# 42 gathered tokens on three partitions each in place of 32 on four, in a hybrid decoder step on one core

## The chip, the cores and the metric

The kernel runs on one core of a Trainium2 chip. The metric is device time in microseconds (us) of one execution. Besides TensorE (PE, with its weight loads as PEld), the core has VectorE (DVE), ScalarE (ACT), GpSimd (POOL) and SyncE (SP), whose queue issues most of the transfers.

## The reference, cut to what matters

264 tokens (256 of a prompt, 8 new ones) go through an input projection, attention and a recurrence, an output projection and a layer norm. That gives x1, 264 tokens by 2048. The change lies in the expert mixer behind it. Each token picks, for each of 8 heads, 16 of 16384 experts, so 128 experts with a weight each:

```
e = take(i1, si // 16) * 128 + take(i2, si % 16)        # 8 heads x 16 experts for a token
g = softmax(sv)
act = gelu(einsum('nd,nhkd->nhk', x, u_tab[e]))
out = einsum('nhk,nhkd->nd', g * act, v_tab[e])
y = layer_norm(alpha * x1 + out)
```

u_tab and v_tab are 16384 x 2048 in float32, 134 MB each.

## The kernel before, in words

The mixer treats the tokens in two ways. The first ND = 232 are dense: both tables are streamed through in 128 blocks of 128 experts, products are made for all experts, and a matrix of gates (zero nearly everywhere) picks the right ones. The last NG = 32 tokens are gathered: each token sits on REP = 4 partitions, and each of these partitions fetches 32 of its token's 128 experts, a half row of 1024 numbers at a time.

**Dense work.** A block is split into a high part `hi` (ACT rounds it, L97) and the rest `lo` (DVE subtracts, L100), in halves of 128x1024. A step s of the main loop does `up(s)` (16 pairs of matmuls: the high weights against x1's high and low parts, L1178, then the low weights against the high part, L1179), and `down(v)` with v = s - 34 (16 such pairs, L1229 and L1230, against the gated activations W). With ND = 232 a pair streams 464 and 232 columns. The high and low parts of x1 lie in `x1s`, 264 columns each, of which `up` reads the first 232 of either.

**Order of a step.** DVE's program order is: sum of the last `up` (`act_sum`, L1188), `lo` of the first half of `down`'s block, four additions into x1 (L1237), `lo` of the second half, gate product (L1205, L1210), `lo` of the first half of the next `up` block, low part of W (L1216), `lo` of its second half, then gathered work. ACT's order is alike; it rounds W behind the gate product (L1212) and the next `up` block behind that. Four pairs of buffers take `hi` and `lo`, six take what the transfers bring.

**Stages.** s = 0 to 5 multiply x1 in float32 without a split (L916), s = 4 to 20 also build the dense gates (L1127), s = 21 to 33 have `up` alone, steps v = 0 to 93 have `up` and `down`, and v = 94 to 127 (`last_step`) have `down` alone, since all 128 `up` blocks are done. The layer norm ends the kernel.

**Gathered work.** `gathered()` is a generator. After each step v, `credit` grows by GRATE, and each whole unit runs the generator to its next `yield`. The first three turns load the expert numbers `exf`, the gates `gat` and the tokens `xrep`, and compute row numbers `eix`. Then each turn issues one indirect transfer of a 128x1024 tile (POOL, L1363) and consumes the tile issued three turns before: for u a product with the token and a sum (`dot`, L1381), then for v a scaled addition (`acc`, L1395). When all is through, 16 matmuls with `selM` add up the partitions of each token (L1400).

Of the kernel before, what the change touches and what calls it, by code (L numbers as in the profile page):

```python
# [18 lines left out]
NC_ = 16  # L19
SEQ = 256  # L20
NB = 8
T = SEQ + NB
NPG = 8
NG = 32
ND = T - NG
REP = 128 // NG
RAWB = 6

SEQS = "qqqqqqqqkkkkkkkkvvvvrrrrrrrrvvvvrrrrrrrr"
# [16 lines left out]
TRATE = 4  # L46
LEAD = 4
GWAIT = 2
GRATE = 1.5
GDELAY = 3  # L50
EPS = 1e-5
LAM0 = 0.8 - 0.6 * math.exp(-0.0)
# [4 lines left out]
def _build(tc, I, O):  # L57
    nc = tc.nc
    ctx = ExitStack()
    PS = bass.MemoryType.PSUM  # L60
    with ctx:
# [50 lines left out]
        def pmisc(shape):  # L112
            return psum.tile(shape, F32, name="misc", bufs=3)
# [65 lines left out]
        iota = cload("iota", [128, 128])  # L179
# [509 lines left out]
        x1, wo = x0, {}  # L689
# [72 lines left out]
        for u in range(2 * NC_):  # L762
# [3 lines left out]
            if u % 2 == 0:  # L766
# [3 lines left out]
                hi, lo = wo.pop(u // 2)  # L770
# [138 lines left out]
        for c in range(NC_):  # L909
            ln.center(c)  # L910

        x1s = big.tile([128, NC_, 2, T], F32R, name="A")
        first = [(ups.pop(k), pmm()) for k in (-16, -15)]

        def native(p, w, c, n=T):
# [14 lines left out]
        Gd = [dram.tile([128, 128, n], F32, name=f"Gd{a}") for a, n in blocks]  # L930
        Ed = dram.tile([SEQ - ND, 128], F32, name="Ed")
        gd = dram.tile([SEQ - ND, 128], F32, name="gd")
        Es = dram.tile([2, 64, 16], F32, name="Es")
        xgd = dram.tile([NG, DM], F32, name="xgd")
        tctx = ExitStack()
        tp_ = pool_in(tctx, "topk", 2)
# [119 lines left out]
        for m in range(2, 16):  # L1056
            k = m - 16
            load_u(k + 2)
            w = ups.pop(k)
            p = pmm()  # L1060
            for i in range(NC_):
                native(p, w, i)
            if m % 2 == 0:
                scores(m // 2 - 1)
            queries(m, p)
            if m < 10:

                for c in range(2 * (m - 2), 2 * (m - 2) + 2):
                    nc.scalar.copy(x1s[:, c, 0], x1[:, c, :])
                    nc.vector.tensor_tensor(x1s[:, c, 1], x1[:, c, :], x1s[:, c, 0], op=OP.subtract)  # L1070
            elif m < 14:
                rows_out(m - 10)

# [9 lines left out]
        def tokens(tt):  # L1083

            i1, i2, g = [a.rearrange("p h k -> p (h k)") for a in (*tops[tt].r, tops[tt].g)]
            tr = []
            for k, a in enumerate((i1, i2, g)):
                p = pmisc([128, 128])
                nc.tensor.transpose(p, a, ident)
                b = tw[0].tile([128, 128], F32, name=f"tr{k}", bufs=1)  # L1090
                nc.scalar.copy(b, p)
                tr.append(b)
            b = tw[0].tile([128, 128], F32, name="tr3", bufs=1)
            nc.scalar.activation(b, tr[1], AF.Copy, scale=-1.0)
            tr.append(b)
            if tt == 1:
                r0 = ND - 128
                ef = tp_.tile([128, 128], F32, name="efp", bufs=1)
                nc.vector.scalar_tensor_tensor(ef, i1, 128.0, i2, op0=OP.mult, op1=OP.add)
                nc.gpsimd.dma_start(Ed, ef[r0:128])  # L1100
                nc.gpsimd.dma_start(gd, g[r0:128])
            yield
            for bk, (a0, n) in enumerate(blocks):
                if a0 // 128 != tt:
                    continue
                st = tw[0].tile([128, 128, n], F32, name="stage")
                for t4 in range(0, n, 4):
                    t0 = a0 % 128 + t4
                    b = tw[0].tile([128, 4, 128], F32, name="gb", bufs=4)
                    if t4 % 8 == 0:  # L1110
                        for q in range(4):
                            nc.scalar.activation(b[:, q, :], iota, AF.Abs, bias=tr[3][:, t0 + q:t0 + q + 1])
                        nc.scalar.activation(b, b, AF.Relu, scale=-1.0, bias=1.0)
                    else:
                        nc.vector.tensor_tensor(b, iota[:, None, :].to_broadcast([128, 4, 128]),
                                                tr[1][:, t0:t0 + 4, None].to_broadcast([128, 4, 128]), op=OP.is_equal)
                    a = tw[0].tile([128, 4, 128], F32, name="ga", bufs=4)
                    for q in range(4):
                        nc.vector.tensor_scalar(a[:, q, :], iota, tr[0][:, t0 + q:t0 + q + 1], tr[2][:, t0 + q:t0 + q + 1],
                                                op0=OP.is_equal, op1=OP.mult)  # L1120
                    if len(prev) == 3:
                        prev.pop(0)()

                    def product(a=a, b=b, st=st, t4=t4, n=n, bk=bk):
                        p = psum.tile([128, 4, 128], F32, name="acc2")
                        for q in range(4):
                            nc.tensor.matmul(p[:, q, :], b[:, q, :], a[:, q, :], start=True, stop=True)  # L1127
                        nc.scalar.copy(st[:, :, t4:t4 + 4], p.rearrange("p t i -> p i t"))
                        if t4 + 4 == n:
                            nc.sync.dma_start(Gd[bk], st)  # L1130

                    prev.append(product)
                    yield

        def gates():
            for tt in range(2):
                yield from tokens(tt)
            while prev:
                prev.pop(0)()
                yield  # L1140

            top = Top(64, 1, "s", ex)
            both([top], [SS], 0)
            yield
            top.less()
            yield
            top.pick(0, 1)
            yield
            top.gate()
            yield  # L1150
            ef = ex.tile([64, 16], F32, name="ef")
            nc.vector.scalar_tensor_tensor(ef, top.r[0][:, 0], 128.0, top.r[1][:, 0], op0=OP.mult, op1=OP.add)
            nc.gpsimd.dma_start(Es[0], ef)
            nc.gpsimd.dma_start(Es[1], top.g[:, 0])


        I["v2"] = I["v"].rearrange("e (a d) -> (e a) d", a=2)
# [9 lines left out]
        def up(k, a=0, b=NC_):  # L1167
            w = ups[k]
            if a == 0:
                pu[k] = pmm([128, 2, ND])  # L1170
            p = pu[k]
            if k < NAT:
                for c in range(a, b):
                    native(p[:, 0], w, c, ND)
                return
            for c in range(a, b):
                hi, lo = w[c // 8]
                nc.tensor.matmul(p, hi[:, c % 8, :], x1s[:, c, :, :ND], start=c == 0, stop=False)  # L1178
                nc.tensor.matmul(p[:, 0, :], lo[:, c % 8, :], x1s[:, c, 0, :ND], start=False, stop=c == NC_ - 1)  # L1179

        def act_sum(k):
            p = pu.pop(k)
# [153 lines left out]
        gp = pool_in(ctx, "gath", 1)  # L1336


        eix = gp.tile([128, 2, NG], I32, name="eix")
        gat = gp.tile([128, NG], F32, name="gat")  # L1340

        def gathered():
            exf = gp.tile([128, NG], F32, name="exf")
            selM = cload("selM", [128, NG], pool=gp)
            xrep = gp.tile([128, DM], F32, name="xrep")
            for r in range(REP):
                a, b, c = r * NG, r * NG + SEQ - ND, (r + 1) * NG
                for k, (d, o) in enumerate(((Ed, exf), (gd, gat))):
                    nc.sync.dma_start(o[a:b], d[:, a:c])
                    nc.sync.dma_start(o[b:c].rearrange("t (h k) -> t h k", k=16),  # L1350
                                      Es[k].rearrange("(h t) k -> t h k", h=8)[:, a // 16:c // 16])
                nc.sync.dma_start(xrep[a:c], xgd)
            for _ in range(GWAIT):
                yield

            nc.vector.tensor_scalar(eix[:, 0], exf, 2.0, None, op0=OP.mult)
            nc.vector.tensor_scalar(eix[:, 1], exf, 2.0, 1.0, op0=OP.mult, op1=OP.add)
            dots = gp.tile([128, 2, NG], F32, name="dots")
            yield

            def rows(tab, a, j):
# [2 lines left out]
                                             in_offset=bass.IndirectOffsetOnAxis(ap=eix[:, a, j:j + 1], axis=0))  # L1364
                return t

            todo = [(j, a) for j in range(NG) for a in range(2)]

            def ahead(tab, use):
                got = []  # L1370
# [11 lines left out]
                                               accum_out=dots[:, a, j:j + 1])  # L1382

            yield from ahead(I["u"], dot)
            wts = gp.tile([128, NG], F32, name="wts")
            nc.vector.tensor_tensor(wts, dots[:, 0], dots[:, 1], op=OP.add)
            nc.scalar.activation(wts, wts, AF.Gelu_apprx_tanh)
            nc.vector.tensor_tensor(wts, wts, gat, op=OP.mult)
# [6 lines left out]
                    nc.vector.scalar_tensor_tensor(accg[:, cols], t, wts[:, j:j + 1], accg[:, cols], op0=OP.mult, op1=OP.add)  # L1395

            yield from ahead(I["v2"], acc)
            pf = pmisc([128, NC_, NG])
            for c in range(NC_):
                nc.tensor.matmul(pf[:, c, :], accg[:, c * 128:(c + 1) * 128], selM, start=True, stop=True)  # L1400
            nc.vector.tensor_tensor(x1[:, :, ND:], x1[:, :, ND:], pf, op=OP.add)

        gg = gathered()
        credit = 0.0
# [51 lines left out]
def _arrays(inp):  # L1456
# [51 lines left out]
    a["cn"] = (to & (g % 2 == 1)[:, None]).astype(f)  # L1508
    a["own"] = (r[:, None] % 32 == np.arange(16)[None, :]).astype(f)
    r = np.arange(128)  # L1510
    a["selM"] = (r[:, None] % NG == np.arange(NG)[None, :]).astype(f)
    return a


# [28 lines left out]
```

## Time and profile before

| what | value |
|---|---|
| median of 3 runs (lowest, highest) | 2092.59 us (2090.44, 2094.37) |
| the profiled execution's own time | 2093.76 us |
| its span, first to last instruction | 2092.0 us |
| busy: PE, PEld, DVE, ACT, POOL | 97%, 88%, 76%, 46%, 11% of the span |
| mean granted TensorE clock | 0.982 of 2.4 GHz; 1.00 in every stretch from 600 to 2000 us |
| DMA | 522 MB, 250 GB/s over the span |

On PE, `down` of v = 0 starts at 918.68 us and that of v = 94 at about 1888 us; `down` ends near 2065 us, and the layer norm closes the kernel. A matmul's recorded duration is longer than its place in the stream, since matmuls overlap in the pipeline; what a matmul costs is read from one start to the next. The same holds for DVE: two operations in a row overlap by about 0.08 us.

### The profile page before, as it was taken

What the parts mean: (1) busy time and instruction counts of PE and PEld (TensorE: products, weight loads), DVE (VectorE), ACT (ScalarE), POOL (GpSimd) and SP (SyncE); (2) the same over time, 40 slices, a digit from 0 to 9 for tenths busy, and PEclk for the clock granted to TensorE, in tenths of its full rate; (3) what the DMA queues carried; (4) which work ended last, traced back from release to release, by engine and by line L of the source; (5) the groups of instructions that cost most, each with busy time, mean ns of one, the idle gap of its engine ahead of it and who ended that gap; (6) DMA issues with size and microseconds to landing.
All of it is one profiled execution on the core that took longest, in us unless ns stands there. A gap on an engine that the chain in (4) does not pass through costs nothing.

```text
span 2092.0 us, 37216 instructions
## 1 busy us (share of the span) xinstructions
PE 2022.8 (97%) x13890; PEld 1835.9 (88%) x13890; DVE 1589.3 (76%) x3245; ACT 969.1 (46%) x1600; POOL 239.6 (11%) x211
## 2 busy tenths in 40 slices
PE   7999899889899999999999999999999999999995
PEld 7888777679788999999999999999999999999995
DVE  5534555665599789667888888888888888878887
ACT  4223554534311599554444444444444444444444
POOL 0000000002400000000111111111222122200014
PEclk9999899989999999999999999999999999999998
DMA  8799488655344477778888888887888888876661
GB/s 282 273 372 319 153 283 305 206 200 180 113 141 142 145 243 242 260 230 321 279 298 302 279 299 293 285 292 251 299 301 280 303 288 289 298 226 222 225 204 62
DMA packets 183623, 522.08 MB, mean 250 GB/s; under 512 B 28858, under 2 KB 61650, under 8 KB 181394
## 3 DMA queue, kind: packets, MB, share of 16 engines
q1 hardware_dynamic: 160400, 451.34, 63.0%
q0 software_dynamic: 18688, 67.41, 9.7%
q8 instruction: 109, 1.79, 0.3%
q10 hardware_dynamic: 4354, 0.96, 0.2%
q14 instruction: 72, 0.59, 0.1%
HBM read 499.65 MB, written 19.97 MB: 248 GB/s over the span
## 4 chain that ended last, share of the span: by engine, by line
PE 79%; DVE 4%; ACT 3%; issue 1%; DMA 1%; POOL 0%; SPq 0%; ACTq 0%; POOLq 0%; DVEq 0%
PE mm L1178 19%; PE acc L1229 18%; PE mm L1179 9%; PE acc L1230 9%; PE mm L916 7%; PE mm L1229 3%; PE acc L1127 2%; PE mm L294 2%; PE acc L632 1%; PE mm L1230 1%; PE mm L295 1%; PE mm L296 1%; PE mm L777 1%; PE misc L373 1%; ACT hi L97 1%
## 5 line engine op out<-in xcount | busy, mean ns | idle before, releaser
L100 DVE TENSOR_TENSOR lo<-raw,hi 128x1024 fp32r<-128x1024 f32 x326 | 397.3, 1225 | 292.8 <-ACT hi L97 287.9
L1178 PE MATMUL mm<-A,hi 128*128 128x464 f32 x1728 | 568.3, 380 | 0.0
L1229 PE MATMUL acc<-w,xl 128*128 128x464 f32 x1640 | 532.7, 376 | 0.0
L1179 PE MATMUL mm<-A,lo 128*128 128x232 f32 x1728 | 465.8, 270 | 0.7 <-DVE lo L100 0.7
L1230 PE MATMUL acc<-w,xl 128*128 128x232 f32 x1640 | 443.0, 270 | 0.0
L97 ACT CAST hi<-raw 128x1024 fp32r<-128x1024 f32 x326 | 329.3, 1045 | 180.1 <-PE mm L295 95.9
L97 ACT CAST xl<-raw 128x1024 fp32r<-128x1024 f32 x260 | 269.1, 1045 | 221.4 <-issue 181.7
L1178 PEld LDWEIGHTS mm<-A,hi 128*128 128x128 f32 x1728 | 324.6, 188 | 42.0
L100 DVE TENSOR_TENSOR xl<-raw,xl 128x1024 fp32r<-128x1024 f32 x260 | 317.3, 1229 | 31.4 <-ACT xl L97 28.8
L1229 PEld LDWEIGHTS acc<-w,xl 128*128 128x128 f32 x1640 | 307.8, 188 | 35.9
L1179 PEld LDWEIGHTS mm<-A,lo 128*128 128x128 f32 x1728 | 330.7, 191 | 0.9 <-DVE lo L100 0.9
L1230 PEld LDWEIGHTS acc<-w,xl 128*128 128x128 f32 x1640 | 312.7, 191 | 0.0
L1212 ACT CAST w<-ac 128x232 fp32r<-128x232 f32 x128 | 49.5, 386 | 335.8 <-DVE ac L1210 335.8
L1237 DVE TENSOR_TENSOR M<-M,acc 128x232 f32<-128x232 f32 x444 | 166.4, 392 | 30.0 <-PE acc L1230 22.4
L916 PE MATMUL mm<-M,raw 128*128 128x264 f32 (+1 forms) x704 | 155.4, 381 | 7.2 <-ACT M L871 7.2
L916 PEld LDWEIGHTS mm<-M,raw 128*128 128x128 f32 x704 | 133.8, 192 | 25.4 <-ACT M L871 7.7
L294 PE MATMUL mm<-xh,hi 128*128 128x264 f32 x448 | 142.0, 317 | 12.4 <-ACT hi L97 6.6
L296 PE MATMUL mm<-xh,lo 128*128 128x264 f32 x448 | 131.5, 294 | 0.5 <-DVE lo L100 0.5
L295 PE MATMUL mm<-xl,hi 128*128 128x264 f32 x448 | 131.1, 293 | 0.2 <-DVE xl L173 0.2
L1363 POOL DMA_INDIRECT ug<-in_u,eix x64 | 79.3, 1239 | 441.3 <-DVE ug L1381 349.2
L1363 POOL DMA_INDIRECT ug<-in_v,eix x64 | 85.8, 1340 | 377.5 <-DVE xrep L1395 308.5
L294 PEld LDWEIGHTS mm<-xh,hi 128*128 128x128 f32 x448 | 88.3, 197 | 42.1 <-issue 28.2
(360 smaller groups left out, 3168.0 us busy)
## 6 DMA issues: line engine op xcount, KB each, us to landing
raw<-in_uT SPq DMA_DIRECT2D x256, 512.0 KB
raw<-in_vt SPq DMA_DIRECT2D x256, 512.0 KB
raw<-in_w_in SPq DMA_DIRECT2D x74, 512.0 KB
cv<-in_ck SPq DMA_DIRECT2D x64, 512.0 KB
cv<-in_cv SPq DMA_DIRECT2D x64, 512.0 KB
raw<-in_wq SPq DMA_DIRECT2D x32, 512.0 KB
Gd<-stage SPq DMA_DIRECT2D x14, 1024.0 KB
gt<-Gd SPq DMA_DIRECT2D x224, 64.0 KB
```

The lines of the kernel that those rows point to most:

```text
L97: nc.scalar.copy(hi, raw)
L100: (eng or nc.vector).tensor_tensor(lo, raw, hi, op=OP.subtract)
L294: nc.tensor.matmul(p, hi, xh[:, c], start=c == 0, stop=False)
L295: nc.tensor.matmul(p, hi, xl[:, c], start=False, stop=False)
L296: nc.tensor.matmul(p, lo, xh[:, c], start=False, stop=c == NC_ - 1)
L916: nc.tensor.matmul(p, w[c // 8][:, c % 8, :], x1[:, c, :n], start=c == 0, stop=c == NC_ - 1)
L1178: nc.tensor.matmul(p, hi[:, c % 8, :], x1s[:, c, :, :ND], start=c == 0, stop=False)
L1179: nc.tensor.matmul(p[:, 0, :], lo[:, c % 8, :], x1s[:, c, 0, :ND], start=False, stop=c == NC_ - 1)
L1229: nc.tensor.matmul(p[:, :, :ND], hi[:, b % 8, :], w, start=i == 0, stop=False)
L1230: nc.tensor.matmul(p[:, 0, :ND], lo[:, b % 8, :], w[:, 0], start=False, stop=i == 7)
L1237: nc.vector.tensor_tensor(a, a, p[:, b, :ND], op=OP.add)
L1363: nc.gpsimd.indirect_dma_start(out=t, out_offset=None, in_=tab, in_offset=bass.IndirectOffsetOnAxis(ap=eix[:, a, j:j + 1], axis=0))
```

## The change

NG becomes 42 and ND 222. Each gathered token sits on three partitions (REP = 128 // 42), which fetch 43, 43 and 42 of its 128 experts; partitions 126 and 127 hold zeros. So the generator has 86 tiles for each table in place of 64, and GRATE goes from 1.5 to 1.7. `x1s` keeps 222 columns only, so that the high and low parts lie side by side.

```
-NG = 32
+NG = 42
 ND = T - NG
 REP = 128 // NG
+NJ = -(-128 // REP)
...
-GRATE = 1.5
+GRATE = 1.7
...
-        x1s = big.tile([128, NC_, 2, T], F32R, name="A")
+        x1s = big.tile([128, NC_, 2, ND], F32R, name="A")
...
-                    t0 = a0 % 128 + t4
+                    t0, w = a0 % 128 + t4, min(4, n - t4)
...
-            nc.gpsimd.dma_start(Es[0], ef)
-            nc.gpsimd.dma_start(Es[1], top.g[:, 0])
+            for k, t in enumerate((ef, top.g[:, 0])):
+                for h in range(8):
+                    nc.gpsimd.dma_start(Es[k][:, h * 16:(h + 1) * 16], t[h * 8:(h + 1) * 8])
...
-                nc.tensor.matmul(p, hi[:, c % 8, :], x1s[:, c, :, :ND], start=c == 0, stop=False)
+                nc.tensor.matmul(p, hi[:, c % 8, :], x1s[:, c], start=c == 0, stop=False)
...
-        eix = gp.tile([128, 2, NG], I32, name="eix")
-        gat = gp.tile([128, NG], F32, name="gat")
+        eix = gp.tile([128, 2, NJ], I32, name="eix")
+        gat = gp.tile([128, NJ], F32, name="gat")
...
+            for t in (exf, gat, xrep):
+                nc.gpsimd.memset(t, 0.0)
...
-            todo = [(j, a) for j in range(NG) for a in range(2)]
+            todo = [(j, a) for j in range(NJ) for a in range(2)]
...
-            pf = pmisc([128, NC_, NG])
-            for c in range(NC_):
-                nc.tensor.matmul(pf[:, c, :], accg[:, c * 128:(c + 1) * 128], selM, start=True, stop=True)
-            nc.vector.tensor_tensor(x1[:, :, ND:], x1[:, :, ND:], pf, op=OP.add)
+            for h in (0, 8):
+                pf = pmisc([128, 8, NG])
+                for c in range(8):
+                    nc.tensor.matmul(pf[:, c, :], accg[:, (h + c) * 128:(h + c + 1) * 128], selM, start=True, stop=True)
+                nc.vector.tensor_tensor(x1[:, h:h + 8, ND:], x1[:, h:h + 8, ND:], pf, op=OP.add)
```

DVE's order at the border between the last step with `up` (v = 93) and the first two of `last_step`, before the change (`mm` and `acc` are PSUM tiles, `M` is x1, `ac` the activations, `gt` the gates, `xl`, `lo` and `hi` parts of weights):

```order
L1216 TENSOR_TENSOR w<-ac,w 128x232
L100 TENSOR_TENSOR lo<-raw,hi 128x1024
L1188 TENSOR_TENSOR ac<-ac,mm 128x232
L1205 TENSOR_TENSOR ac<-ac,gt 128x224
L1210 TENSOR_TENSOR ac<-ac,gt 128x8
L1237 TENSOR_TENSOR M<-M,acc_20614 128x232 x2
L1237 TENSOR_TENSOR M<-M,acc_20631 128x232 x2
L1216 TENSOR_TENSOR w<-ac,w 128x232
L100 TENSOR_TENSOR xl<-raw,xl 128x1024 x2
```

And the same place on DVE after the change (`xrep<-ug,wts,xrep` is the scaled addition of a gathered tile):

```order
L1218 TENSOR_TENSOR w<-ac,w 128x222
L101 TENSOR_TENSOR lo<-raw,hi 128x1024
L1400 SCALAR_TENSOR_TENSOR xrep<-ug,wts,xrep 128x1024
L1190 TENSOR_TENSOR ac<-ac,mm 128x222
L1207 TENSOR_TENSOR ac<-ac,gt 128x208
L1212 TENSOR_TENSOR ac<-ac,gt 128x14
L1239 TENSOR_TENSOR M<-M,acc_20626 128x222 x2
L1239 TENSOR_TENSOR M<-M,acc_20643 128x222 x2
L1218 TENSOR_TENSOR w<-ac,w 128x222
L101 TENSOR_TENSOR xl<-raw,xl 128x1024 x2
L1400 SCALAR_TENSOR_TENSOR xrep<-ug,wts,xrep 128x1024 x2
```

Before, the gathered additions are over by v = 91 and none stands behind it; now they go on into `last_step`: two, two and one by turns in v = 94 to 106, 22 in all.

PE's order at the end of the gathered work, before (the 16 matmuls with `selM` stand behind `down(91)`, and an `up` follows):

```order
L1229 MATMUL acc_20420<-w,xl 128x2x232
L1230 MATMUL acc_20420<-w,xl 128x232
L1400 MATMUL misc<-c_selM,xrep 128x32 x16
L1178 MATMUL mm<-A,hi 128x464
L1179 MATMUL mm<-A,lo 128x232
```

And PE after the change (behind `down(107)`, and `down(108)` follows):

```order
L1231 MATMUL acc_21478<-w,xl 128x2x222
L1232 MATMUL acc_21478<-w,xl 128x222
L1406 MATMUL misc<-c_selM,xrep 128x42 x16
L1231 MATMUL mm<-w,hi 128x2x222
L1232 MATMUL mm<-w,lo 128x222
```

The sums over partitions moved from a step with `up` into the stretch without, and every matmul of a pair lost 20 or 10 columns.

## Rows read from the trace of the kernel before

**Rows 1.** Busy time of the engines by stretch (from:to, length, engines, clock, DMA share, GB/s)

```profile
1000.00:1400.00 400.00, 400.00 (x2482) 371.31 (x2481) 340.14 (x580) 190.82 (x273) 72.43 (x58) 1.00 0.86 293
1430.00:1840.00 410.00, 410.00 (x2542) 380.45 (x2541) 350.49 (x537) 195.80 (x279) 79.92 (x60) 1.00 0.86 292
1886.00:2047.00 161.00, 161.00 (x1003) 149.98 (x1003) 137.09 (x264) 70.73 (x88) 8.60 (x7) 1.00 0.64 214
```

**Rows 2.** Timeline of PE (start us, duration, instruction): borders of up and down

```profile
1326.71 0.38 PE L1178 MATMUL mm<-A,hi 128*128 128x464 f32 x1
...
1843.24 0.38 PE L1178 MATMUL mm<-A,hi 128*128 128x464 f32 x1
...
1848.32 0.27 PE L1179 MATMUL mm<-A,lo 128*128 128x232 f32 x1
1848.43 0.38 PE L1229 MATMUL acc<-w,xl 128*128 128x464 f32 x1
...
1853.56 0.38 PE L1178 MATMUL mm<-A,hi 128*128 128x464 f32 x1
```

**Rows 3.** Who waited for whom, 1000 to 1700 us (total us, times, longest)

```profile
DVE lo L100 <- ACT hi L97: 95.4, 68, 1.5
```

**Rows 4.** Timeline of DVE over one step with two dots (idle before in brackets)

```profile
1320.05 0.38 DVE L1205 TENSOR_TENSOR ac<-ac,gt 128x224 f32<-128x224 f32 x1
...
1321.92 1.23 DVE L100 TENSOR_TENSOR lo<-raw,hi 128x1024 fp32r<-128x1024 f32 x1 [1.40 <-ACT hi L97]
...
1324.51 1.22 DVE L1381 SCALAR_TENSOR_TENSOR ug<-ug,xrep 128x1024 f32<-128x1024 f32 x1
...
1325.65 1.22 DVE L1381 SCALAR_TENSOR_TENSOR ug<-ug,xrep 128x1024 f32<-128x1024 f32 x1
...
1326.80 0.39 DVE L1188 TENSOR_TENSOR ac<-ac,mm 128x232 f32<-128x232 f32 x1
...
1330.85 0.38 DVE L1205 TENSOR_TENSOR ac<-ac,gt 128x224 f32<-128x224 f32 x1
```

**Rows 5.** Timeline of DVE over one step with two scaled additions

```profile
1464.78 0.38 DVE L1205 TENSOR_TENSOR ac<-ac,gt 128x224 f32<-128x224 f32 x1
...
1469.22 2.48 DVE L1395 SCALAR_TENSOR_TENSOR xrep<-ug,wts,xrep 128x1024 f32<-128x1024 f32 x2
1471.62 0.39 DVE L1188 TENSOR_TENSOR ac<-ac,mm 128x232 f32<-128x232 f32 x1
...
1475.67 0.38 DVE L1205 TENSOR_TENSOR ac<-ac,gt 128x224 f32<-128x224 f32 x1
```

**Rows 6.** Timeline of DVE over one step of down alone

```profile
1989.31 0.38 DVE L1205 TENSOR_TENSOR ac<-ac,gt 128x224 f32<-128x224 f32 x1
...
1991.12 0.82 DVE L1237 TENSOR_TENSOR M<-M,acc 128x232 f32<-128x232 f32 x2 [0.61 <-PE acc L1230]
...
1994.44 0.38 DVE L1205 TENSOR_TENSOR ac<-ac,gt 128x224 f32<-128x224 f32 x1
```

**Rows 7.** Groups of PE instructions, 600 to 850 us (busy us, mean ns)

```profile
L1127 PE MATMUL acc<-ga,gb 128*128 128x128 f32 x464 | 57.0, 276 | 1.0 <-ACT stage L1128 1.0
...
L916 PE MATMUL mm<-M,raw 128*128 128x232 f32 x192 | 38.4, 360 | 0.0
```

**Rows 8.** Timeline of PE: the matmuls with selM, and what follows

```profile
1863.87 3.66 PE L1400 MATMUL misc<-c_selM,xrep 128*128 128x32 f32 x32
1867.36 0.45 PE L1178 MATMUL mm<-A,hi 128*128 128x464 f32 x1
```

**Rows 9.** Timeline of DVE: the row numbers of the gathered experts

```profile
934.43 0.18 DVE L1356 TENSOR_SCALAR eix<-exf 128x32 int32<-128x32 f32 x1 [2.38 <-DMA gat<-Es]
```

**Rows 10.** Groups of POOL instructions (busy us, mean ns)

```profile
L715 POOL MEMSET M<- 128x2080 f32 x1 | 1.8, 1847 | 12.0 <-DVE xl L173 12.0
```

**Rows 11.** Busy time by stretch: the input projection's transfers

```profile
100.00:200.00 100.00, 100.00 (x1233) 85.14 (x1231) 41.77 (x89) 24.20 (x50) 0.00 (x0) 1.00 0.96 346
```

**Rows 12.** Transfers 1000 to 1700 us, median us from issue to landing

```profile
ug<-in_u,eix POOLq DMA_INDIRECT x54, 6.9
```

More of the change, by code (lines that the diff above doesn't have):

```diff
@@ L932, in _build @@
         gd = dram.tile([SEQ - ND, 128], F32, name="gd")
-        Es = dram.tile([2, 64, 16], F32, name="Es")
+        Es = dram.tile([2, NB, 128], F32, name="Es")
         xgd = dram.tile([NG, DM], F32, name="xgd")
@@ L1068, in _build @@
                 for c in range(2 * (m - 2), 2 * (m - 2) + 2):
-                    nc.scalar.copy(x1s[:, c, 0], x1[:, c, :])
-                    nc.vector.tensor_tensor(x1s[:, c, 1], x1[:, c, :], x1s[:, c, 0], op=OP.subtract)
+                    nc.scalar.copy(x1s[:, c, 0], x1[:, c, :ND])
+                    nc.vector.tensor_tensor(x1s[:, c, 1], x1[:, c, :ND], x1s[:, c, 0], op=OP.subtract)
             elif m < 14:
@@ L1107, in tokens @@
                 for t4 in range(0, n, 4):
-                    t0 = a0 % 128 + t4
+                    t0, w = a0 % 128 + t4, min(4, n - t4)
                     b = tw[0].tile([128, 4, 128], F32, name="gb", bufs=4)
                     if t4 % 8 == 0:
-                        for q in range(4):
+                        for q in range(w):
                             nc.scalar.activation(b[:, q, :], iota, AF.Abs, bias=tr[3][:, t0 + q:t0 + q + 1])
-                        nc.scalar.activation(b, b, AF.Relu, scale=-1.0, bias=1.0)
+                        nc.scalar.activation(b[:, :w], b[:, :w], AF.Relu, scale=-1.0, bias=1.0)
                     else:
-                        nc.vector.tensor_tensor(b, iota[:, None, :].to_broadcast([128, 4, 128]),
-                                                tr[1][:, t0:t0 + 4, None].to_broadcast([128, 4, 128]), op=OP.is_equal)
+                        nc.vector.tensor_tensor(b[:, :w], iota[:, None, :].to_broadcast([128, w, 128]),
+                                                tr[1][:, t0:t0 + w, None].to_broadcast([128, w, 128]), op=OP.is_equal)
                     a = tw[0].tile([128, 4, 128], F32, name="ga", bufs=4)
-                    for q in range(4):
+                    for q in range(w):
                         nc.vector.tensor_scalar(a[:, q, :], iota, tr[0][:, t0 + q:t0 + q + 1], tr[2][:, t0 + q:t0 + q + 1],
@@ L1122, in tokens, with product @@
                         prev.pop(0)()
-                    def product(a=a, b=b, st=st, t4=t4, n=n, bk=bk):
+                    def product(a=a, b=b, st=st, t4=t4, w=w, n=n, bk=bk):
                         p = psum.tile([128, 4, 128], F32, name="acc2")
-                        for q in range(4):
+                        for q in range(w):
                             nc.tensor.matmul(p[:, q, :], b[:, q, :], a[:, q, :], start=True, stop=True)
-                        nc.scalar.copy(st[:, :, t4:t4 + 4], p.rearrange("p t i -> p i t"))
-                        if t4 + 4 == n:
+                        nc.scalar.copy(st[:, :, t4:t4 + w], p[:, :w].rearrange("p t i -> p i t"))
+                        if t4 + w == n:
                             nc.sync.dma_start(Gd[bk], st)
@@ L1177, in up @@
                 hi, lo = w[c // 8]
-                nc.tensor.matmul(p, hi[:, c % 8, :], x1s[:, c, :, :ND], start=c == 0, stop=False)
-                nc.tensor.matmul(p[:, 0, :], lo[:, c % 8, :], x1s[:, c, 0, :ND], start=False, stop=c == NC_ - 1)
+                nc.tensor.matmul(p, hi[:, c % 8, :], x1s[:, c], start=c == 0, stop=False)
+                nc.tensor.matmul(p[:, 0, :], lo[:, c % 8, :], x1s[:, c, 0], start=False, stop=c == NC_ - 1)
         def act_sum(k):
@@ L1336, in _build @@
         gp = pool_in(ctx, "gath", 1)
-        eix = gp.tile([128, 2, NG], I32, name="eix")
-        gat = gp.tile([128, NG], F32, name="gat")
+        eix = gp.tile([128, 2, NJ], I32, name="eix")
+        gat = gp.tile([128, NJ], F32, name="gat")
         def gathered():
-            exf = gp.tile([128, NG], F32, name="exf")
+            exf = gp.tile([128, NJ], F32, name="exf")
             selM = cload("selM", [128, NG], pool=gp)
             xrep = gp.tile([128, DM], F32, name="xrep")
+            for t in (exf, gat, xrep):
+                nc.gpsimd.memset(t, 0.0)
             for r in range(REP):
[L1347 to L1352, printed above, removed]
+                a, b, e = r * NG, r * NG + SEQ - ND, (r + 1) * NG
+                c, d = r * NJ, min((r + 1) * NJ, 128)
+                for k, (i, o) in enumerate(((Ed, exf), (gd, gat))):
+                    nc.sync.dma_start(o[a:b, :d - c], i[:, c:d])
+                    nc.sync.dma_start(o[b:e, :d - c], Es[k][:, c:d])
+                nc.sync.dma_start(xrep[a:e], xgd)
             for _ in range(GWAIT):
@@ L1357, in gathered @@
             nc.vector.tensor_scalar(eix[:, 1], exf, 2.0, 1.0, op0=OP.mult, op1=OP.add)
-            dots = gp.tile([128, 2, NG], F32, name="dots")
+            dots = gp.tile([128, 2, NJ], F32, name="dots")
             yield
@@ L1384, in gathered @@
             yield from ahead(I["u"], dot)
-            wts = gp.tile([128, NG], F32, name="wts")
+            wts = gp.tile([128, NJ], F32, name="wts")
             nc.vector.tensor_tensor(wts, dots[:, 0], dots[:, 1], op=OP.add)
@@ L1510, in _arrays @@
     r = np.arange(128)
-    a["selM"] = (r[:, None] % NG == np.arange(NG)[None, :]).astype(f)
+    a["selM"] = (r[:, None] % NG == np.arange(NG)[None, :]).astype(f) * (r[:, None] < NG * REP).astype(f)
     return a
```

## The prediction

> **What bounds the kernel now.** I read the busy times by stretch first. From 1000 to 1840 us PE has no idle time at full clock: 2482 matmuls in 400 us, 2542 in 410 us, 0.161 us each in both [rows 1]. So PE paces the main stage. But DVE is at 85% there, and the next question is what its other 15% are. The list of waits answers it: in 68 steps DVE's idle time has essentially one place, `lo` of the next `up` block, 1.40 us each time [rows 3]. In DVE's order this wait stands behind the gate product: ACT must first round W from that product, then round the weights, and only then can DVE subtract. DVE's own order makes this wait, and it does not shrink when PE gets faster. So I count it as DVE time.
>
> A step with two dots then takes DVE 1330.85 - 1320.05 = 10.80 us, of which the dots are 1326.80 - 1324.51 = 2.29 us, 1.145 each [rows 4]. A step with two scaled additions takes 10.89 us, and these are 2.40 us of it, 1.20 each [rows 5]. Either way 8.50 us are left for a step without gathered work. At 1.5 gathered tiles a step, DVE needs 8.50 + 1.5 x 1.145 = 10.22 us, or 10.30 with scaled additions. PE needs 5.19 us for `up` (1843.24 to 1848.43) and 5.13 for `down` (to 1853.56), together 10.32 [rows 2]. **DVE has 0.02 to 0.1 us to spare in a step of 10.32.** The 97% of PE hide a second engine at the limit.
>
> In the steps of `down` alone DVE goes round in 5.13 us and waits for PE 0.61 of them [rows 6], so it has 4.5 us of work.
>
> **The change on PE.** By columns a third of a pair's 0.3206 us (5.13 / 16) belongs to the low weights: 0.107, and the rows show 0.11 from 1848.32 to 1848.43 [rows 2]. The high part takes the other 0.2136. For the latter 464 columns become 444: 0.2136 x 444 / 464 = 0.2045. Whether the low part gains is open. Nearest row: 32 matmuls of only 32 columns, with a 128-column weight load each, are (1867.36 - 1863.87) / 32 = 0.109 apart [rows 8]. So a weight load for each matmul alone holds them that far apart, and the 232-column matmul already stands there. I take no gain, 0.107; the other end, by columns, is 0.102. The Trainium skill (TensorE: Matmul & The Clock Gate, section LDWEIGHTS) gives a float32 weight load one column per 1/1.2 ns, whatever streams beside it; that speaks against any gain below 128 / 1.2 = 106.7 ns, and by it the low part stays and the sum is the one below.
>
> A pair becomes 0.3115 us, 16 of them 4.98. `down` saves 0.15. `up` costs 0.06 more than `down` now; its two runs of 232 columns become one run of 444, as W always was, so I give it 4.98 too, a saving of 0.21 (0.15 if the run was not the reason). A full step needs PE 9.96 us.
>
> **The change on DVE.** Six operations a step lose 10 of 232 columns, the gate product 2 of 232 net. At 1.145 us for 1024 columns [rows 4] that is 62 x 1.1 ns = 0.07 us, and with ACT's narrower W 0.08: 8.50 becomes 8.42. At 1.7 tiles a step DVE needs 8.42 + 1.7 x 1.145 = 10.37 us with dots and 10.46 with scaled additions. That is more than PE's 9.96. **In steps with gathered work DVE sets the pace, and PE's gain there is lost.**
>
> **The sum, stage by stage** (turns of the generator: 1.7 (v + 1), rounded down; 3 for the set-up, 86 + 3 for u, 86 + 3 for v):
> - s = 0 to 5: 192 matmuls of 0.20 us [rows 7], 10 of 232 columns fewer: -1.7 us.
> - Dense gates: 20 of 464 matmuls fewer (ten tokens, two passes), in a stage where PE is busy throughout: 20 x 0.11 = -2.2, at the spacing of [rows 8] (57.0 / 464 = 0.12 by [rows 7]).
> - s = 6 to 33: 28 `up` by 0.21: -5.9.
> - v = 0 to 3, where nothing is consumed yet: 4 x (10.32 - 9.96) = -1.4.
> - v = 4 to 93: 86 dots and 64 scaled additions. DVE: 90 x 8.42 + 86 x 1.145 + 64 x 1.20 = 757.8 + 98.5 + 76.8 = 933.1. It enters with a lead: a second half ready at 1330.85 is needed by `down` from 1326.71 + 5.19, after 4 pairs, at 1333.2 [rows 2, 4], so 2.3 us. Net 930.8 against 90 x 10.32 = 928.8: +2.0.
> - v = 94 to 106: the last 22 scaled additions meet steps in which DVE has 4.5 - 0.07 = 4.43 us of work. 13 x 4.43 + 22 x 1.20 = 84.0, against 13 x 5.14 = 66.8 now, where there is no gathered work: +17.2, the dearest term.
> - v = 108 to 127: PE paces again, 20 x 0.15 = -3.0. The matmuls with `selM` (3.5 us) are paid before and after.
>
> The sum is -14.2 + 2.0 + 17.2 = **+5.0 us**. The profiled execution has 2093.76 us (a span of 2092.0 and 1.8 around it) and becomes 2098.8; it stood 1.2 over the median of its runs, so I expect a median near 2097.6, rounded to 2098.
>
> Edits at nothing. The clearing of `xrep` on POOL: a clear of the same width took 1.8 us [rows 10], and POOL has nothing else between the sample gates and the first gathered tile, so it runs early; uncovered, SP's loads of `exf` and the weights behind them would wait those 1.8 us. Loading `exf`, `gat`, `xrep` takes 15 issues in place of 20, so the 2.38 us for which DVE waits for them [rows 9] can only shrink; PE does not feel them now, since no gathered work follows for two steps. The 16 small `Es` transfers go out long before they are read. POOL's 22 more indirect transfers for either table land in 6.9 us [rows 12], while a tile is issued three turns, some 11 us even in the short steps, before its use.
>
> **Rivals.**
> 1. The low part follows its columns after all (0.1023): 0.075 less for each of 28 `up`, 20 `down`, and 0.15 for each of four full steps, about -4.2: median 2093.5, no change. Against it: [rows 8]. DVE's stage stays as it is.
> 2. DVE does not set the pace in the full steps, because its 1.40 us wait shrinks when it is pressed (ACT rounding the weights before W is due, for instance). Then v = 4 to 93 take 90 x 9.96 = 896.4, so -32.4 in place of +2.0, and the lead of 2.3 is there for the last stretch: about 2061, clearly faster. It decides once DVE's step falls from 10.4 under 9.96, which takes 0.44 off the wait. Against it: 95.4 / 68 is exactly 1.40, with a longest wait of 1.5 [rows 3], so it is the same length whether DVE is early or late.
> 3. DMA becomes the bound. A full step moves 2.10 MB of weights, 1.7 x 0.52 of gathered rows and 0.11 of gates, 3.1 MB; in 10.4 us that is 298 GB/s, against 293 at a share of 0.86 now [rows 1]. In the short steps it is 2.05 MB in 6.5 us, 317 GB/s. Where transfers are only large the core got 346 at 0.96 [rows 11]. If 293 were the limit, full steps would take 10.6 us (+19) and short ones 7.0 (+7): about 2124. It decides where 298 GB/s are not reached; the share of 0.86 speaks against that.
>
> **Chances and range.** The forecast 0.50 (2094 to 2104 by its own bounds: `up` without its run +1.7 and up to 3 us either way for the lead and for DVE's work of 4.5, read as 5.13 - 0.61), rival 1 0.20, rival 2 0.12, rival 3 0.10, and 0.08 for what I don't see. Less than 0.2% (4.2 us) is what a measurement of this kernel can hardly tell from no change. Of the forecast's half some 0.38 lie over 2096.8 and 0.12 within; rival 1 is within, with a corner below; rival 3 and half of the unseen are slower. That gives faster 0.19, same 0.30, slower 0.51. The range leaves out rival 2 and the far part of rival 3: 2087 to 2112.
>
> **What the profile of the changed kernel would show.** In v = 4 to 93: a mean step of 10.35 to 10.45 us, DVE's idle time still 1.40 in one place, and matmuls with gaps before L1181 or L1232, released by DVE's `lo`, some 0.4 us a step. Starts from a 444 to a 222 matmul 0.205 apart, and 0.107 from the 222 to the next; 0.102 there means rival 1. In v = 94 to 106: steps of 5.6 and 6.8 us by turns with DVE at its limit; then steps of 4.98. Steps of 9.96 with gathered work in them would prove rival 2, gathered tiles for which DVE waits, or weights for which ACT waits, rival 3. The forecast is wrong if DVE's step is shorter than its present parts add up to, or if the lead carried over into v = 94 is much over 2.3 us.

## The result, and the profile after

The changed kernel takes **2104.83 us** (median of 5 runs, 2103.22 to 2105.89), the kernel before 2093.35 beside it (5 runs, 2090.44 to 2096.06): a ratio of 1.0059, interval 1.0047 to 1.0071. It is slower, by 11.5 us, and lies within the range of 2087 to 2112, though 0.8 us over the bounds that the forecast gave itself (2094 to 2104). One execution of the kernel before at the higher rate (2820.9 us, at a granted clock of 0.65) is left out of its median below. The profiled execution has 2105.58 us and a span of 2103.8, against 2092.0: the ledger below has to add up to +11.8, where the forecast's sum had +5.0.

First the stretches of the kernel after (from:to, length, busy us and counts of PE, PEld, DVE, ACT, POOL, granted clock, DMA share, GB/s):

```profile
837.10:842.00 4.90, 2.94 (x19) 2.54 (x17) 4.53 (x17) 2.41 (x5) 0.00 (x0) 0.99 1.00 365
842.00:847.00 5.00, 3.44 (x12) 3.25 (x13) 3.81 (x9) 1.58 (x4) 1.22 (x3) 0.50 0.63 185
849.00:853.00 4.00, 4.00 (x28) 3.82 (x27) 1.15 (x2) 1.49 (x3) 3.28 (x7) 1.00 0.85 289
...
1000.00:1400.00 400.00, 396.45 (x2473) 369.59 (x2473) 344.31 (x596) 186.01 (x269) 99.81 (x66) 1.00 0.88 300
1430.00:1840.00 410.00, 405.51 (x2532) 378.40 (x2531) 350.66 (x549) 191.47 (x279) 96.87 (x65) 1.00 0.87 297
1890.00:1960.00 70.00, 59.36 (x352) 52.34 (x351) 69.24 (x118) 25.03 (x33) 25.82 (x18) 1.00 0.90 311
1970.00:2060.00 90.00, 90.00 (x587) 86.42 (x586) 77.42 (x145) 38.56 (x47) 8.33 (x7) 1.00 0.65 212
```

Where [rows 1] had no idle time on PE, its two stretches now have 3.6 and 4.5 us of it, and PE does 2473 shorter matmuls in 400 us where it did 2482 longer ones. From 1890 to 1960 DVE is busy 69.24 us of 70 and PE 59.36: DVE is the bound there, in the open. From 1970 on PE has no gap again.

Who waits for whom from 1000 to 1700 us (total us, times, longest), with the same place as in [rows 3] and a new one on PE:

```profile
DVE lo L101 <- ACT hi L98: 93.4, 67, 1.5
PEld acc L1232 <- DVE xl L101: 13.6, 41, 0.4
PEld acc L1231 <- issue: 10.3, 25, 0.5
PE acc L1231 <- DVE M L1239: 1.1, 6, 0.3
```

PE now waits 0.3 to 0.4 us at a time for DVE's low half in `down`. A second wait stands at the first matmul of `down`, whose accumulator DVE must first have added into x1 (L1239): six of these are put down to DVE, and for 25 weight loads ("issue") the profile names nobody. DVE still idles 93.4 / 67 = 1.39 us, in one place.

The chain that ended last, by engine (PE had 79% of it before, DVE 4%):

```profile
PE 56%; DVE 21%; issue 4%; DMA 3%; ACT 3%; SPq 1%; POOL 0%; DVEq 0%; ACTq 0%; POOLq 0%
```

DVE's timeline after: the top-16 of the new tokens (833 to 842 us), a step with two dots, and the short steps:

```profile
830.99 2.36 DVE L101 TENSOR_TENSOR lo<-raw,hi 128x1024 fp32r<-128x1024 f32 x2 [4.06 <-ACT hi L98]
833.27 0.38 DVE L1190 TENSOR_TENSOR ac<-ac,mm 128x222 f32<-128x222 f32 x1
833.56 0.47 DVE L942 MAX8 vs<-SS 64x8 f32<-64x128 f32 x2
...
841.96 0.41 DVE L994 TENSOR_REDUCE r1s<-eqs 64x16 f32<-64x256 f32 x1
842.29 2.34 DVE L101 TENSOR_TENSOR xl<-raw,xl 128x1024 fp32r<-128x1024 f32 x2
...
1327.99 0.37 DVE L1207 TENSOR_TENSOR ac<-ac,gt 128x208 f32<-128x208 f32 x1
...
1329.84 1.23 DVE L101 TENSOR_TENSOR lo<-raw,hi 128x1024 fp32r<-128x1024 f32 x1 [1.39 <-ACT hi L98]
...
1338.71 0.37 DVE L1207 TENSOR_TENSOR ac<-ac,gt 128x208 f32<-128x208 f32 x1
...
1917.55 0.37 DVE L1207 TENSOR_TENSOR ac<-ac,gt 128x208 f32<-128x208 f32 x1
...
1923.13 0.37 DVE L1207 TENSOR_TENSOR ac<-ac,gt 128x208 f32<-128x208 f32 x1
...
1927.51 2.48 DVE L1400 SCALAR_TENSOR_TENSOR xrep<-ug,wts,xrep 128x1024 f32<-128x1024 f32 x2
1929.90 0.37 DVE L1207 TENSOR_TENSOR ac<-ac,gt 128x208 f32<-128x208 f32 x1
```

The two-dot step of [rows 4] went from 10.80 to 1338.71 - 1327.99 = 10.72 us. The short steps with one and two scaled additions take 5.58 and 6.77 us, where 5.6 and 6.8 were expected, and none of their rows has an idle time in brackets.

And PE's timeline at the borders of the stages:

```profile
839.67 0.37 PE L1180 MATMUL mm<-A,xl 128*128 128x444 f32 x1
843.56 0.56 PE L1181 MATMUL mm<-A,xl 128*128 128x222 f32 x1 [3.52 <-DVE xl L101]
843.91 0.60 PE L1180 MATMUL mm<-A,xl 128*128 128x444 f32 x1
...
844.49 0.60 PE L1180 MATMUL mm<-A,xl 128*128 128x444 f32 x1
...
848.58 0.46 PE L1180 MATMUL mm<-A,xl 128*128 128x444 f32 x1
...
850.86 0.37 PE L1180 MATMUL mm<-A,hi 128*128 128x444 f32 x1
...
870.59 0.38 PE L1180 MATMUL mm<-A,xl 128*128 128x444 f32 x1
870.81 0.27 PE L1181 MATMUL mm<-A,xl 128*128 128x222 f32 x1
870.91 0.37 PE L1180 MATMUL mm<-A,hi 128*128 128x444 f32 x1
...
916.04 0.37 PE L1231 MATMUL acc<-w,xl 128*128 128x444 f32 x1
...
956.07 0.37 PE L1231 MATMUL acc<-w,xl 128*128 128x444 f32 x1
...
1877.33 0.44 PE L1231 MATMUL acc<-w,xl 128*128 128x444 f32 x1 [0.26 <-DVE M L1239]
...
1970.84 0.43 PE L1406 MATMUL misc<-c_selM,xrep 128*128 128x42 f32 x3
...
1974.34 0.45 PE L1231 MATMUL mm<-w,hi 128*128 128x444 f32 x1
```

The starts of `down(0)`, `(4)`, `(93)` and `(108)`, 916.04, 956.07, 1877.33 and 1974.34, cut the program into stages (before: 918.68, 960.10, 1882.93 and 1960.08; `up(6)`, the first that is split, went from 717.46 to 715.65). The 3.5 us of `selM` are taken out of both kernels' stages here; they change place and cancel.

| stage | before | after | difference | forecast |
|---|---|---|---|---|
| to `up(6)` | 717.46 | 715.65 | -1.8 | -1.7 |
| `up(6)` to `down(0)` | 201.22 | 200.39 | **-0.8** | **-8.1** |
| `down(0)` to `down(4)` | 41.4 | 40.0 | -1.4 | -1.4 |
| `down(4)` to `down(93)` | 919.33 | 921.26 | +1.9 | +2.0 |
| `down(93)` to `down(108)` | 77.15 | 93.51 | +16.4 | +17.2 |
| to the end of the span | 131.92 | 129.46 | -2.5 | -3.0 |

One row is out, the second. At 839.67 us an `up` begins that ends at 850.86, 11.19 us in place of 5.01. (The first expectation below counts from the middle of the `up` before, 837 us, and so has 10.8 us for it.) The timeline shows why: behind its first matmul PE stands still for 3.52 us, until DVE's low half comes, which DVE does at 842.29, behind 8.7 us of top-16 work in one piece. Then its pairs are 844.49 - 843.91 = 0.58 us apart instead of 0.31, up to 848.6: the granted clock in that stretch is 0.50, that is 1.2 GHz, and back at 1.00 from 849 on. So 11.19 - 5.01 = 6.2 us were lost: 3.7 by the wait (843.56 - 839.67, less the 0.21 that a high matmul takes), and 2.5 by the clock that fell in it. The Trainium skill (TensorE: Matmul & The Clock Gate, section What's actually happening) says that activity is what releases the throttle; the trace agrees, with 0.50 right behind the 3.52 us and 1.00 after some 5 us of matmuls. In the short steps, with waits of up to 1.0 us on PE, the clock stayed at 1.00. In four runs below whose order is the same up to here (the lower rate, half the columns, two runs, the moved line) the wait is 3.5 us as well, and the `up` takes 10.36 to 11.34 us, as the clock comes back sooner or later; their stage from `up(6)` to `down(0)` takes 199.1 to 200.4 us.

### The profile page after: what moved, and what is told of

The parts are those of the page before. It is cut to its first block, busy times and chain, and to the rows that moved or that the text cites. A ratio compares the mean times of both kernels' runs of the same rounds, so it can differ in the third digit from the quotient of the medians.

```text
span 2103.8 us, 37309 instructions
## 1 busy us (share of the span) xinstructions
PE 2003.1 (95%) x13870; PEld 1829.1 (87%) x13870; DVE 1624.2 (77%) x3301; ACT 957.4 (46%) x1593; POOL 340.4 (16%) x272
## 4 chain that ended last, share of the span: by engine, by line
PE 56%; DVE 21%; issue 4%; DMA 3%; ACT 3%; SPq 1%; POOL 0%; DVEq 0%; ACTq 0%; POOLq 0%
PE mm L1180 11%; PE acc L1231 11%; PE mm L917 7%; PE acc L1232 6%; DVE xl L101 6%; PE mm L1181 6%; DVE lo L101 4%; DVE xrep L1400 3%; DVE M L1239 2%; PE acc L1128 2%; DVE ug L1386 2%; PE mm L295 1%; PE mm L1231 1%; PE acc L633 1%; DMA gt<-Gd 1%
## 5 line engine op out<-in xcount | busy, mean ns | idle before, releaser
L1180 PE MATMUL mm<-A,hi 128*128 128x444 f32 x1728 | 549.1, 374 | 0.0
L1231 PE MATMUL acc<-w,xl 128*128 128x444 f32 x1640 | 524.4, 375 | 5.9 <-issue 3.8
L1181 PE MATMUL mm<-A,lo 128*128 128x222 f32 x1728 | 456.0, 264 | 0.0
L1232 PE MATMUL acc<-w,xl 128*128 128x222 f32 x1640 | 438.8, 268 | 3.1
L1214 ACT CAST w<-ac 128x222 fp32r<-128x222 f32 x128 | 48.5, 379 | 341.1 <-DVE ac L1212 341.1
L1368 POOL DMA_INDIRECT ug<-in_u,eix x86 | 128.4, 1493 | 465.1 <-DVE ug L1386 382.0
L1368 POOL DMA_INDIRECT ug<-in_v,eix x86 | 128.7, 1497 | 376.8 <-DVE xrep L1400 317.1
L1239 DVE TENSOR_TENSOR M<-M,acc 128x222 f32<-128x222 f32 x444 | 162.3, 383 | 17.6 <-PE acc L1232 9.9
L1194 ACT ACTIVATE ac<-ac 128x222 f32<-128x222 f32 x122 | 47.7, 391 | 242.1 <-DVE ac L1190 242.1
```

Source lines behind the costliest of these rows:

```text
L1180: nc.tensor.matmul(p, hi[:, c % 8, :], x1s[:, c], start=c == 0, stop=False)
L1181: nc.tensor.matmul(p[:, 0, :], lo[:, c % 8, :], x1s[:, c, 0], start=False, stop=c == NC_ - 1)
L1231: nc.tensor.matmul(p[:, :, :ND], hi[:, b % 8, :], w, start=i == 0, stop=False)
L1232: nc.tensor.matmul(p[:, 0, :ND], lo[:, b % 8, :], w[:, 0], start=False, stop=i == 7)
L1239: nc.vector.tensor_tensor(a, a, p[:, b, :ND], op=OP.add)
L1368: nc.gpsimd.indirect_dma_start(out=t, out_offset=None, in_=tab, in_offset=bass.IndirectOffsetOnAxis(ap=eix[:, a, j:j + 1], axis=0))
```

## The experiments

The runs with the later chain, with another rate alone and with half the columns were timed beside the kernel before at 2093.5 us; those with the moved line alone, with two runs of columns, and the first of the last two beside 2092.82; the chain in pieces and the last one beside 2092.57.

**Is it where the top-16 stands?** The whole chain two turns of the side work later:

```
+            for _ in range(2):
+                yield
             top = Top(64, 1, "s", ex)
             both([top], [SS], 0)
```

> The changed kernel with two empty turns ahead of the new tokens' top-16 work, so that it stands in DVE's order where it stood before the change. Theory (in the stage of the dense gates the two groups that fell away let DVE's top-16 chain of some 8.7 us move ahead of the low halves that up(21) waits for): the step at 837 us falls from 10.8 to about 5 to 6 us, and the kernel from 2104.8 to about 2099. Rival (PE waits there for something else, such as PSUM or ACT, which came with narrower groups): the long step stays, 2105.

Measured: 2105.3 us (ratio 1.0057, 1.0044 to 1.0070), no gain. The loss only moved: two `up` of 7.48 and 7.73 us, from 838.14 to 853.35, 5.2 over two normal ones. Of this kernel the wait there, and the stretch behind it:

```profile
PEld mm L1182 <- ACT hi L98: 2.2, 1, 2.2
```

```profile
846.00:851.00 5.00, 4.21 (x17) 3.92 (x17) 3.61 (x5) 3.03 (x5) 4.54 (x10) 0.66 0.87 269
```

PE now waits for ACT's high half instead, 1.9 us, and then 0.8 for DVE's low half, and the clock falls again. ACT itself was late behind the chain: the activation ahead of that rounding had waited 1.69 us for DVE's sum of the last `up`, which stands behind the picks. DVE's order itself is that of the kernel before again, with a low half between the top-16 and the picks:

```profile
837.05 0.41 DVE L950 FIND_INDEX8 sis<-svs,combs 64x8 uint32<-64x256 f32 x1
837.39 2.33 DVE L101 TENSOR_TENSOR xl<-raw,xl 128x1024 fp32r<-128x1024 f32 x2
...
840.42 0.42 DVE L991 TENSOR_TENSOR eqs<-sfs,c_iota 64x256 f32<-64x256 f32 x1
```

So the theory that the chain only stands at a bad place fell.

**Is it that the chain comes in one piece?** Same work, cut into 16 pieces and dealt out behind every third turn of the dense gates:

```
         def gates():
+            new = sample()
             for tt in range(2):
-                yield from tokens(tt)
+                for n, _ in enumerate(tokens(tt)):
+                    if n % 3 == 2:
+                        next(new, None)
+                    yield
...
+        def sample():
             top = Top(64, 1, "s", ex)
-            both([top], [SS], 0)
-            yield
+            for sets in (top.halves(SS), None):
+                if sets is None:
+                    sets = top.sums(0)
+                    yield
+                for i in range(5):
+                    top16(sets, i)
+                    yield
```

> The changed kernel with the new tokens' top-16 work cut into 16 pieces, one behind every third group of the dense gates, in place of one stretch of some 10 us on DVE behind the last group. Theory (moving that stretch by two turns only moved the wait, because PE, with fewer gate matmuls and shorter up matmuls, now reaches up(21) and up(22) before DVE has done that stretch and their low halves): no long step near 840 us, PE's 5.0 us throughout, and 5 us less, about 2099.5. Rival (DVE has no room in the stage of the dense gates either): the steps there lengthen by as much, 2104 to 2105.

Measured: 2100.23 us (1.0034, 1.0022 to 1.0046), 4.6 under the change; the stage from `up(6)` to `down(0)` takes 195.9 us in place of 200.4. The same stretch of it:

```profile
837.10:842.00 4.90, 4.90 (x33) 4.69 (x32) 0.61 (x3) 2.13 (x5) 0.00 (x0) 1.00 0.99 369
842.00:847.00 5.00, 5.00 (x33) 4.78 (x32) 2.75 (x4) 2.62 (x5) 0.00 (x0) 1.00 0.56 171
```

PE has no gap, the clock stays at 1.00, and the `up` from 834 us on take 5.01 to 5.03 us. Not all 6.2 come back: the pieces stretch two steps of the gate stage near 800 us, by 1.8 us in all.

**Does DVE really have no room in a full step?** The kernel before, whose PE needs 10.32 us, with the GRATE of the change:

```
-GRATE = 1.5
+GRATE = 1.7
```

> The kernel before with GRATE 1.7 in place of 1.5 and nothing else. Theory (DVE was 0.02 to 0.1 us a step from setting the pace): v = 4 to 80 need DVE 77 x 8.50 + 64 x 1.145 + 64 x 1.20 = 804.6 us against PE's 794.6; less a lead of 2.3, the kernel is 7 to 8 us slower, about 2101, with PE waiting for DVE's low halves in these steps. Rival (PE paced and had room beside it): no change, 2093.

Measured: 2101.87 us (1.0033, 1.0020 to 1.0046), +8.4. Its waits from 1000 to 1700 us and its first stretch:

```profile
DVE lo L100 <- ACT hi L97: 95.6, 68, 1.5
PEld acc L1230 <- DVE xl L100: 6.0, 19, 0.3
```

```profile
1000.00:1400.00 400.00, 399.73 (x2463) 368.52 (x2462) 339.99 (x580) 188.90 (x272) 92.43 (x62) 1.00 0.86 295
```

With 0.2 tiles more a step PE waits for DVE in the kernel before too, and does 2463 matmuls where [rows 1] has 2482. The bound of DVE stands without any change on PE.

**Less gathered work in a full step.** The change, with GRATE 1.55:

```
-GRATE = 1.7
+GRATE = 1.55
```

> The changed kernel with GRATE 1.55 in place of 1.7. Theory (DVE's work sets the pace wherever gathered tiles are consumed): v = 4 to 93 consume 136 tiles in place of 150 and take 17 us less, v = 94 to 116 consume 36 and need 23 x 4.43 + 36 x 1.20 = 145 us, against 134 for the same steps at 1.7: in sum 5 to 6 us faster, about 2099. Rival (a gathered tile costs in the short steps because transfers arrive late there): more of them in the short steps cost at least as much, 2105 or more.

Measured: 2099.05 us (1.0026, 1.0017 to 1.0035), 5.8 under the change though more tiles are left for the short steps:

```profile
1000.00:1400.00 400.00, 398.95 (x2517) 376.30 (x2516) 341.80 (x591) 190.45 (x275) 95.90 (x61) 1.00 0.87 297
```

**DVE or DMA?** All transfers stay, but of every second half row DVE takes in 64 of its 1024 columns. This leaves out about half of the gathered products and sums:

```
-                        use(got.pop(0), j, a, slice(a * 1024, (a + 1) * 1024))
+                        use(got.pop(0), j, a, 64 if a else 1024)
...
```

> The changed kernel with all its transfers, but of the second half row of each expert (but the first) only 64 of 1024 columns are consumed on DVE, which leaves out nearly half of the gathered arithmetic. Theory (DVE sets the pace with gathered work): full steps need DVE 8.42 + 1.7 x (0.58 + 0.08) = 9.5 us and fall to PE's 10.0, v = 94 to 106 come near PE's 5.0 too; in sum some 40 us less, about 2062. Rival (transfers or POOL set the pace): nothing changes, 2105.

Measured: 2062.05 us (0.9853, 0.9839 to 0.9868), with steps of 10.00 and 10.02 us:

```profile
1000.00:1400.00 400.00, 399.86 (x2556) 382.13 (x2555) 323.32 (x611) 192.55 (x278) 81.94 (x67) 1.00 0.90 310
```

With every transfer in place PE runs free at 310 GB/s, above the 300 of the change. DMA is not the bound.

**What makes DVE's 1.40 us?** ACT rounds the first half of the next weights before W, and not behind it:

```
             W[k] = epool[0].tile([128, 2, ND], F32R, name="w", bufs=17)
-            nc.scalar.copy(W[k][:, 0], ac)
+            if not behind:
+                nc.scalar.copy(W[k][:, 0], ac)
...
-                gate_mult(k)
+                gate_mult(k, True)
             d, n = (ups, s + 1) if s + 1 < 128 else (downs, v + 1)
-            split1(d, n, 0)
+            d[n][0] = split1_(d[n][0], None, (lambda: nc.scalar.copy(W[k][:, 0], acts[k])) if k >= 0 else None)
```

> The changed kernel with one line of ACT's order moved: the rounding of W stands behind the rounding of the next block's first half. Theory (DVE's 1.40 us wait is made by that order and counts as DVE time): the wait nearly goes, DVE needs some 9.1 us in a full step, PE paces with 10.0, and v = 4 to 93 take 30 us less; v = 94 to 106 gain a little from a longer lead: about 2072. Rival (DMA or POOL are at their limit as well): less than half of that, 2090 or more.

Measured: 2069.95 us (0.9889, 0.9872 to 0.9905), faster than both kernels. Its wait and its first stretch:

```profile
DVE lo L101 <- ACT hi L98: 44.5, 70, 0.7
```

```profile
1000.00:1400.00 400.00, 400.00 (x2560) 382.75 (x2559) 357.83 (x617) 203.44 (x280) 90.86 (x68) 1.00 0.89 311
```

The wait is halved, 0.64 us a step, and PE has no gap. So some 0.76 of the 1.40 us were made by the order of two instructions on ACT. The rest costs nothing here, as PE paces; whether it could go too was not tested.

**The same line moved in the kernel before**, where ACT's order is the same:

```
-                gate_mult(k)
+                gate_mult(k, True)
...
```

> The kernel before with the same line of ACT's order moved. Theory (PE paces there at 10.32 us a step, DVE just under it): no change, 2093. Rival (PE's step is already stretched by DVE in places): faster by more than 4 us.

Measured: 2092.7 us (1.0001, 0.9991 to 1.0011): nothing, as PE paces there.

**Is the one run of 444 columns why `up` gets faster?** The change, with the parts 264 columns apart again:

```
-        x1s = big.tile([128, NC_, 2, ND], F32R, name="A")
+        x1s = big.tile([128, NC_, 2, T], F32R, name="A")[:, :, :, :ND]
```

> The changed kernel with the high and low parts of x1 again 264 columns apart, so that an up matmul reads two runs of 222 columns. If the run is what made an up pair longer than a down pair before, the start-to-start time of the high matmul in up rises by about 3 ns from 212 and up from 5.01 to 5.06 us, seen in the steps of up alone; the kernel's time stays within noise, 2105. If not, up stays at 5.01.

One execution: 2101.98 us, and in the trace `up` takes 5.01 to 5.03 us (5.00 to 5.02 with the change). A high matmul follows 0.213 us after its predecessor, against 0.212. The run is worth some 1 ns a matmul, not the 3 that I had expected. Why `up` took 0.03 to 0.06 us more than `down` before stays open.

**All together.** First the later chain, the moved line and a higher rate:

```
-GRATE = 1.7
+GRATE = 1.95
...
+            for _ in range(2):
+                yield
...
-                gate_mult(k)
+                gate_mult(k, True)
```

> The changed kernel with the two empty turns, the moved line and GRATE 1.95, at which all gathered work ends by v = 92. Theory: DVE needs 9.3 us in a full step, PE paces with 10.0 throughout and with 5.0 in the short steps: about 2051. Rival (transfers): a full step moves 3.2 MB, 323 GB/s at 10.0 us; if 300 GB/s are the most, 10.8 us a step, 2120.

Measured: 2055.96 us (0.9824, 0.9808 to 0.9840), 5 more than expected: the two long `up` are still in it, 7.48 and 7.73 us from 839 us on, as the first experiment had shown. Its first stretch:

```profile
1000.00:1400.00 400.00, 400.00 (x2561) 382.76 (x2560) 366.04 (x633) 204.02 (x282) 106.88 (x77) 1.00 0.92 323
```

323 GB/s, and still no gap on PE. Then the chain in pieces in place of the later one, the rest the same:

```
-GRATE = 1.7
+GRATE = 1.95
...
+            new = sample()
...
-                gate_mult(k)
+                gate_mult(k, True)
```

> The run with the moved line and GRATE 1.95, with the spread top-16 work in place of the two empty turns. Theory: the 5 us of the waits near 840 us come off 2056: about 2051. Rival: no gain, 2056.

Measured: **2052.38 us** (0.9799, 0.9784 to 0.9814), 40 us under the kernel before.

## Why the prediction was right, and where its size was off

**Direction and bound: right.** DVE paces the full steps in the mean once PE needs 10.0 us: PE waits for its low halves as expected, and beside that, unforeseen, at the first matmul of `down`; 1.40 us of idle time are still there, and the stage came out at +1.9 against +2.0. One reading in DVE's part was wrong: the gate product lost 10 columns, not 2 (224 + 8 became 208 + 14), which is 0.01 us a step. The step with two dots fell by the 0.08 us of the forecast all the same. Taking gathered work from DVE (2062 us) or its idle time (2070 us) frees it each time.

**The dearest term: right.** The 22 scaled additions in the short steps cost 16.4 us, against 17.2, with DVE busy 99% of that stretch.

**The step that failed** is "s = 6 to 33: 28 `up` by 0.21: -5.9", together with the -2.2 of the dense gates. The gains came: in this stage an `up` went from 5.18 to 5.01 us in the mean, 28 of them are -4.7, and twenty gate matmuls fewer, at 0.11 each, gave about -2.2. But 6.2 us went at 840 to 851 us, where the kernel before lost 1.0 (PE waited 0.66 us there, and the clock stayed at 1.00). Another 0.9 went in short pauses of the gate stage: -4.7 - 2.2 + 5.2 + 0.9 = -0.8, as measured. I had called that stage one in which PE is busy throughout, and had not asked what covers DVE's top-16 once each `up` is 0.17 shorter and the gate matmuls end earlier. Before, a low half stood between the top-16 and the picks, and PE waited once. DVE and PE of the kernel before:

```profile
841.57 0.41 DVE L949 FIND_INDEX8 sis<-svs,combs 64x8 uint32<-64x256 f32 x1
841.90 2.33 DVE L100 TENSOR_TENSOR xl<-raw,xl 128x1024 fp32r<-128x1024 f32 x2
...
844.95 0.42 DVE L990 TENSOR_TENSOR eqs<-sfs,c_iota 64x256 f32<-64x256 f32 x1
...
851.43 0.38 PE L1179 MATMUL mm<-A,lo 128*128 128x232 f32 x1 [0.66 <-DVE lo L100]
```

Now both stand in one piece of 8.7 us. That this work costs the time is shown by the experiment that deals it out over the gate stage (4.6 us back). That it is not the missing low half between is shown by the one that moves it: DVE's order there is that of before, and 5.2 us are lost all the same. So PE's work beside it no longer covers it. DVE had also stood idle for 4.06 us just ahead of the piece, waiting for ACT's high half (830.99); by these times the low half would have come early enough without that. The wait alone costs nothing: with the chain in pieces 3.80 us of it are still there, and PE has no gap. No run took this wait away. How much the shorter `up` did and how much the missing gate matmuls was not told apart either.

**The low part: the premise was wrong, the sum held.** From a 222 matmul to the next start it is 870.91 - 870.81 = 0.10 us (0.101 in the mean), not 0.107: it follows its columns, as rival 1 had it, and as the end by columns (0.102) said. The Trainium skill (TensorE: Matmul & The Clock Gate, section LDWEIGHTS) has a weight load take P / 1.2 ns for P columns, by estimate 106.7 ns for 128. As a floor between two starts, as the prediction took it, that does not hold here: 0.101 us were measured, with a load of 128 columns for each matmul. The `selM` matmuls still stand (1974.34 - 1970.84) / 32 = 0.109 apart, so [rows 8] were no floor for these; they were matmuls of plain float32. But the high part takes 0.212 and not 0.2045, and the two errors cancel: a pair has 0.313, forecast 0.3115, a full step without waits 10.00 to 10.02 us, forecast 9.96.

**The rivals.** Rival 1 had its mechanism and not its time, as a pair is not shorter. Rival 2 did not come by itself: the wait is as long as before, but moving one instruction does what it describes. Rival 3 fell: 298 GB/s were called for, 300 came, and the chip gave 323.

**The early stage.** The -1.8 to `up(6)` is within what differs from one execution to the next: kernels equal up to there began `up(6)` between 710.6 and 716.3 us. The float32 matmuls of [rows 7] show the gain themselves, 36.8 us in place of 38.4.

## What to carry to other kernels

Where one engine is busy 97% of the time, count for the next one what it needs in a step with the waits that its program order makes; if that is within 1% of the step, a gain on the first is lost. Then look at how such a wait is made: here two instructions of a third engine, exchanged, were worth 35 us in the changed kernel and nothing in the kernel before. And where a stage gets shorter, look for the longest piece of other work on the engine that feeds it: the stage may no longer be long enough to cover it, and if the clock falls in the wait, more is paid than the wait: here 6.2 us for 3.7.

## What the runs showed of the hardware that was not expected

A wait of 3.52 us on PE cost 2.5 us more behind it, at a granted clock of 0.50; behind waits of up to 1.0 us in the short steps the clock stayed at 1.00. Waits of 1.9 and 0.8 us with half a us of matmuls between them, in the run with the later chain, were followed by 0.50 as well. And the clock can fall where PE does not wait: right behind the 32 `selM` matmuls it was 0.50 for a few us in three of the twelve traces and 1.00 in the others. Of the last run of all, where it cost some 1.6 us:

```profile
1851.50:1854.50 3.00, 3.00 (x12) 2.81 (x11) 2.93 (x10) 2.45 (x4) 0.00 (x0) 0.50 0.02 5
```

Behind the start of a 222-column matmul with rounded operands the next start came after 0.101 us, with a weight load of 128 columns for each, while float32 matmuls of 42 columns stood 0.109 apart. The transfers reached 323 GB/s with small gathered rows among them, without a wait on PE.
